# Queries and keys of a hybrid decoder trunk, transposed by VectorE blocks and a DRAM tile in place of TensorE

## The chip, the cores and the metric

The kernel runs on one core of a Trainium2 chip. The metric is the device time of one execution in microseconds (us); lower is better. The core has five engines with instruction queues of their own: TensorE (PE in the profile, its weight loads PEld), VectorE (DVE), ScalarE (ACT), GpSimd (POOL) and SyncE (SP). SP only issues DMAs here.

## The reference, cut to what matters

Two layers, each feed-forward, mixer, feed-forward, over 256 tokens of width 1024, all in float32. The part that the change touches is the attention of the mixer: eight heads of 128 columns.

```python
q, k, v, z, xbc, dt_raw, u, vg, gate_raw = jnp.split(xn @ w_in, split_at, axis=-1)
qt = (q * (dh ** -0.5)).transpose(0, 2, 1, 3)
...
s_own = jnp.einsum('bhqd,bhkd->bhqk', qb, k_own).astype(F32)
s_own = jnp.where(dist_own >= 0,
                  s_own - slopes[:, None, None] * dist_own.astype(F32), -jnp.inf)
...
p = jax.nn.softmax(scores, axis=-1).astype(vt.dtype)
```

With 256 tokens there is one key block, so the attention is plain causal attention with a distance penalty. The other two branches of the mixer are a state-space scan (SSD, 16 heads in two groups, chunks of 128 tokens) and a gated unit; the three are gated, projected and summed.

## The kernel before

**Tiling.** Tokens come in two tiles of 128 (`t` = 0, 1). Weights stream from DRAM in 496 blocks of 128 x 1024 float32 (`load`, line 160, into tile `raw`), six of them ahead. Each block is split by ACT into a rounded part `whi` (line 180) and by DVE into a rest `wlo` (line 181), eleven blocks ahead of their use, and each product is made of three matmuls (lines 213 to 215). Weights and their split take part in every stage, so a DVE instruction that stands still holds the splits behind it.

**Order.** A matrix product (`gemm`) issues its matmuls in a fixed order; after each piece it calls `pump` with that piece's time, and `tick` advances small side tasks (generators), each of which sleeps a number of microseconds from the table `W` after every `yield`. So the order of the instructions on every engine is fixed when the program is built. Each engine executes its own queue in order; an instruction that waits holds all behind it.

**The mixer around the change.** Products run in the order xbc, z, q (2 chunks of 512 columns), k (2 chunks), v (2 chunks), then the gates. `qk_evac` (line 730) is the side task of a q or k chunk: ACT copies the two 128 x 512 results out of PSUM into tiles `qtok` (line 504), and `transposed` (line 508) makes four TensorE transposes a token tile into a PSUM tile `ctr` (line 513), which ACT copies into `qT` or `kT` (line 516). The result has the head's 128 columns on partitions and the tokens along the free axis. Attention multiplies them (line 760, `qk`).

At the same time the scan runs (`ssd`, line 651). For each token tile and group it makes, per quarter of the heads, a weight tile `ssw`: a matmul `seg` (line 680), a DVE add (682), four ACT exponentials (686), a DVE product (688). Then eight matmuls `yd` (711) use two such tiles, and DVE adds their result to `y` (714, 722). `scaled` scales the values `xs` on DVE (671). After both groups `to_parts` transposes `y` on TensorE (`xtr`, 300), and DVE and ACT make the parts `xg`, `ysh`, `ysl` (314, 316, 317).

**Buffers.** Tiles of 128 x 512 come from one pool of six buffers, tag `b2` (line 54: `B4, B2 = 16, 6`). While the scan runs, three of the six are held throughout: `acsr` (the running sums, line 622), `btok` (line 560) and `cbt` (line 658). `qtok`, `ssw`, `xg` and the small helpers share the other three. When none is free, the next instruction that needs one waits for the last reader of the buffer that it is given. PSUM tiles of tag `tr` (`ctr`, `seg`, `yd`, `state`, `xtr`, `qk`) share three banks.

**What the feed-forward stages do.** There `swap_out` (line 275) lets DVE transpose every 32 x 32 block of a 128 x 512 tile in place (line 277, tile `xt`) and writes it to a DRAM tile; `swap_in` (line 282) reads it back with four DMAs that put the blocks where a whole transpose would have them. The weight columns are reordered on the host (`_woven`) so that each piece that is read is 128 floats long.

Of the kernel before, what the change touches and what calls it, by code (L numbers as in the profile page):

```python
# [9 lines left out]
F32 = mybir.dt.float32  # L10
# [6 lines left out]
P = 128  # L17
L = 2
S = 256
NT = S // P  # L20
# [31 lines left out]
def trunk(ctx, tc, a):  # L52
    nc = tc.nc
    V, A, G, T = nc.vector, nc.scalar, nc.gpsimd, nc.tensor
# [5 lines left out]
    dram = ctx.enter_context(tc.tile_pool(name="dram", bufs=1, space=bass.MemoryType.DRAM))  # L60
# [3 lines left out]
    def b4(name, shape=(P, 1024), dt=F32):  # L64
        return big.tile(list(shape), dt, name=name, tag="b4", bufs=B4)
# [216 lines left out]
    def swap_in(dst, rd):  # L282

        v = rd.rearrange("(a i) (c e) -> c i a e", a=4, c=4)
        for c in range(4):
            nc.sync.dma_start(dst[32 * c:32 * c + 32], v[c])

    def halves(ps, hi, lo):

# [188 lines left out]
    def mixer(l, x, r2, nxt):  # L478
# [29 lines left out]
        def transposed(toks, place, eng):  # L508

            for t in range(NT):  # L510
                ps = tr("ctr")
                for j in range(4):
                    T.transpose(ps[:, j * P:(j + 1) * P], toks[t][:, j * P:(j + 1) * P], ident)
                p3 = ps.rearrange("p (k t) -> p k t", k=4)
                if eng == "a":
                    A.copy(place(t), p3)
                else:
                    V.tensor_copy(place(t), p3)
                yield W["tr"]
# [208 lines left out]
        qk = {}  # L728

        def qk_evac(which, c, ps):  # L730
            toks = tokens(ps, rq if which == "q" else r2, "qtok")
            o = b4(f"{which}T", (P, 4, S))
            qk[which, c] = o
            yield W["qk"]
            yield from transposed(toks, lambda t: o[:, :, t * P:(t + 1) * P], "a")

        vv = {}

# [7 lines left out]
        def attention(yax, free):  # L746
            for t in range(NT):
                while t and not free:
                    yield 0
                n = (t + 1) * P  # L750
# [3 lines left out]
                for g in range(2):  # L754
                    sc[g] = (b4 if t else b2)("sc", (P, 4, n))
                    for u in range(0, 4, per):
                        ps = tr("qk")
                        for j in range(per):
                            hh = u + j
                            T.matmul(ps[:, j * n:(j + 1) * n], qk["q", g][:, hh, t * P:(t + 1) * P],  # L760
                                     qk["k", g][:, hh, 0:n], start=True, stop=True)
                        for j in range(per):
                            hh = u + j
                            V.scalar_tensor_tensor(sc[g][:, hh, :], alibi[t], 2.0 ** -(4 * g + hh + 1),
                                                   ps[:, j * n:(j + 1) * n], op0=ALU.mult, op1=ALU.add)
                        yield W["qs"]
                    V.reduce_max(mx[:, 4 * g:4 * g + 4], sc[g], axis=AX.X)
# [3 lines left out]
                for g in range(2):  # L771
                    for j in range(4):
                        c = slice(4 * g + j, 4 * g + j + 1)
# [7 lines left out]
                for g in range(2):  # L781
# [11 lines left out]
                    for j in range(4):  # L793
                        hh = 4 * g + j
# [187 lines left out]
    x, r2 = XT("x"), {}  # L982
# [73 lines left out]
def _woven(w, n):  # L1056

    v = w.reshape(*w.shape[:-1], -1, n // P, 4, 32)
    return np.ascontiguousarray(v.swapaxes(-3, -2)).reshape(w.shape)
# [27 lines left out]
def _arrays(i):  # L1087
    f = {k: np.ascontiguousarray(v, dtype=np.float32) for k, v in i.items()}
    w = f["w_in"]
    cut = np.cumsum([0, 1024, 1024, 1024, 1024, 1536, 16, 1024, 1024, 1024, 1024, 1024])  # L1090
    q, k, v, z, xbc, dt, u, vg, g0, g1, g2 = (w[:, :, s:e] for s, e in zip(cut[:-1], cut[1:]))
    order = [xbc, z, q, k, v, g1, f["p_ssm"], vg, g0, f["p_attn"], u, g2, f["p_sgu"], f["w_out"]]
    mix = [_chunks(m).reshape(L, -1, P, 1024) for m in order]
    col = lambda m: m.reshape(L, -1, P).transpose(0, 2, 1)
    par = np.concatenate(
        [col(f["ffn1_pre_g"]), col(f["mix_pre_g"]), col(f["ffn2_pre_g"]), col(f["ssm_norm_g"]),
         f["conv_w"].reshape(L, 4, CT, P).transpose(0, 3, 2, 1).reshape(L, P, 48),
         col(f["conv_b"]), f["sgu_b"].transpose(0, 2, 1)], axis=2)
    return {
        "x": f["x"].reshape(S, D),  # L1100
        "con": _constants(),
        "par": par.transpose(1, 0, 2),
        "hpar": np.stack([f["dt_bias"], f["a_log"], f["d_skip"]], axis=1),
        "gu1": _gated(f["ffn1_w_gu"]),
        "dn1": f["ffn1_w_down"].reshape(L, KF, P, D),
        "gu2": _gated(f["ffn2_w_gu"]),
        "dn2": f["ffn2_w_down"].reshape(L, KF, P, D),
        "mix": np.concatenate(mix, axis=1),
        "wdt": dt.reshape(L, KD, P, SH).transpose(0, 2, 1, 3).reshape(L, P, KD * SH),
        "sgw": f["sgu_w"].transpose(0, 1, 3, 2),  # L1110
        "ffn1_post_g": f["ffn1_post_g"],
        "mix_post_g": f["mix_post_g"],
        "ffn2_post_g": f["ffn2_post_g"],
        "sgu_ln_g": f["sgu_ln_g"],
        "sgu_ln_b": f["sgu_ln_b"],
    }
# [18 lines left out]
```

## Time and profile before

| | |
|---|---|
| median of 3 runs | 1486.49 us (1485.8 to 1487.09) |
| the profiled execution | 1487.98 us, of which the span of its instructions is 1486.2 us |
| PE busy | 1472.1 us, 99% of the span |
| PEld busy | 1218.8 us, 82% |
| DVE busy | 955.2 us, 64% |
| ACT busy | 782.6 us, 53% |
| POOL busy | 55.6 us, 4% |
| mean granted TensorE clock | 0.997 |
| DMA | 293.37 MB, mean 197 GB/s |

The span runs from the first to the last instruction of one profiled execution. A share of busy time is an average over stages; what holds the work up in one stage is read from the waits and the chain of that stage. In a row of a timeline stand start, time, engine, line, operation, output<-inputs, shapes, and in brackets the idle time of the engine before it with what ended that. An instruction of one engine can begin a little before the one ahead of it has ended, since they are pipelined, so distances from start to start count.

### The profile page before, as it was taken

To read this page: it belongs to the slowest core of one execution; us is meant where nothing else is said; L and a number is where in the kernel's file an instruction comes from. 1 tells how busy PE (TensorE), PEld (TensorE's weight loads), DVE (VectorE), ACT (ScalarE), POOL (GpSimd) and SP (SyncE) were. 2 spreads that over 40 slices of the span, in tenths; PEclk is the share of its full clock that TensorE was granted. 3 is DMA by queue.
4 is the path that set the end of the run, shared out by engine and by line. 5 is a ranking of instruction groups with operands and counts; after the bars stand their busy time and mean duration, and the time that the engine had idled before them with its cause. 6 is when DMAs were issued, how large, how long until landed. Compare 5 with 4: busy or idle time off the path is not lost.

```text
span 1486.2 us, 18786 instructions
## 1 busy us (share of the span) xinstructions
PE 1472.1 (99%) x6850; PEld 1218.8 (82%) x6850; DVE 955.2 (64%) x1160; ACT 782.6 (53%) x1079; POOL 55.6 (4%) x98
## 2 busy tenths in 40 slices
PE   9999999999999999999999999999999999999998
PEld 7888888878888888888888888888788888888886
DVE  6766477766666857656486564876665667676652
ACT  6644367555374536544364543765554645464441
POOL 0000020000000000000000000200000000000000
PEclk9999999999999999999999999999999999999999
DMA  8987655335556445888568784654354564478860
GB/s 291 323 253 236 199 190 179 127 115 184 159 181 217 168 154 198 283 230 259 163 230 256 235 253 132 224 167 135 119 192 141 194 204 170 134 272 261 238 200 29
DMA packets 112476, 293.37 MB, mean 197 GB/s; under 512 B 16896, under 2 KB 41600, under 8 KB 112384
## 3 DMA queue, kind: packets, MB, share of 16 engines
q1 hardware_dynamic: 111808, 291.84, 60.6%
q8 instruction: 54, 0.88, 0.2%
q10 hardware_dynamic: 576, 0.33, 0.1%
q14 instruction: 38, 0.31, 0.1%
HBM read 279.54 MB, written 12.58 MB: 197 GB/s over the span
## 4 chain that ended last, share of the span: by engine, by line
PE 94%; DVE 4%; ACT 1%; issue 1%; POOL 0%; DMA 0%; DVEq 0%; ACTq 0%; POOLq 0%
PE gu L213 11%; PE gu L215 11%; PE gu L214 11%; PE dn L213 5%; PE dn L215 5%; PE dn L214 5%; PE br L213 3%; PE br L215 3%; PE br L214 3%; PE gate L215 2%; PE gate L213 2%; PE gate L214 2%; DVE wlo L181 2%; PE xbc L215 1%; PE xbc L213 1%; PE xbc L214 1%
## 5 line engine op out<-in xcount | busy, mean ns | idle before, releaser
L181 DVE TENSOR_TENSOR wlo<-raw,whi 128x1024 fp32r<-128x1024 f32 x495 | 600.2, 1232 | 331.1 <-ACT whi L180 319.8
L180 ACT CAST whi<-raw 128x1024 fp32r<-128x1024 f32 x495 | 512.8, 1051 | 380.9 <-PE gu L215 131.8
L213 PE MATMUL gu<-whi,xh 128*128 128x512 f32 x704 | 276.0, 392 | 1.4 <-ACT xh L316 1.4
L214 PE MATMUL gu<-wlo,xh 128*128 128x512 f32 x704 | 274.9, 391 | 0.0
L215 PE MATMUL gu<-whi,xl 128*128 128x512 f32 x704 | 274.8, 390 | 0.0
L213 PEld LDWEIGHTS gu<-whi,xh 128*128 128x128 f32 x704 | 132.7, 188 | 29.8 <-ACT xh L316 1.8
L215 PEld LDWEIGHTS gu<-whi,xl 128*128 128x128 f32 x704 | 132.6, 188 | 28.0 <-DVE xl L317 0.4
L214 PEld LDWEIGHTS gu<-wlo,xh 128*128 128x128 f32 x704 | 132.5, 188 | 27.9 <-DVE wlo L169 0.9
L213 PE MATMUL dn<-whi,hTh 128*128 128x512 f32 x352 | 137.5, 391 | 0.0
L215 PE MATMUL dn<-whi,hTl 128*128 128x512 f32 x352 | 137.0, 389 | 0.0
L214 PE MATMUL dn<-wlo,hTh 128*128 128x512 f32 x352 | 136.9, 389 | 0.0
L215 PEld LDWEIGHTS dn<-whi,hTl 128*128 128x128 f32 x352 | 66.1, 188 | 13.8
L213 PE MATMUL gate<-whi,xh 128*128 128x512 f32 x192 | 77.3, 403 | 0.0
L214 PEld LDWEIGHTS dn<-wlo,hTh 128*128 128x128 f32 x352 | 66.1, 188 | 13.5
L213 PEld LDWEIGHTS dn<-whi,hTh 128*128 128x128 f32 x352 | 66.1, 188 | 13.4
L215 PE MATMUL gate<-whi,xl 128*128 128x512 f32 x192 | 75.0, 391 | 0.0
L214 PE MATMUL gate<-wlo,xh 128*128 128x512 f32 x192 | 74.8, 390 | 0.0
L316 ACT CAST xh<-xg 128x512 fp32r<-128x512 f32 (+1 forms) x25 | 15.1, 603 | 62.3 <-DVE xg L314 62.3
L215 PEld LDWEIGHTS gate<-whi,xl 128*128 128x128 f32 x192 | 36.0, 188 | 7.7
L405 ACT ACTIVATE silu<-gu,r 128x512 f32<-128x512 f32 (+1 forms) x48 | 31.3, 654 | 19.8 <-PE gu L215 16.2
L214 PEld LDWEIGHTS gate<-wlo,xh 128*128 128x128 f32 x192 | 36.2, 188 | 6.6
L213 PEld LDWEIGHTS gate<-whi,xh 128*128 128x128 f32 x192 | 36.1, 188 | 6.6
(243 smaller groups left out, 2248.3 us busy)
## 6 DMA issues: line engine op xcount, KB each, us to landing
raw<-in_mix SPq DMA_DIRECT2D x232, 512.0 KB, 4.2
raw<-in_gu SPq DMA_DIRECT2D x175, 512.0 KB, 4.9
raw<-in_dn SPq DMA_DIRECT2D x88, 512.0 KB, 4.5
swap<-xt SPq DMA_DIRECT2D x40, 256.0 KB, 3.2
hr<-swap SPq DMA_DIRECT2D x160, 64.0 KB, 4.9
row_ffn_post_g<-in_ffn_post_g SPq DMA_DIRECT2D x4, 512.0 KB, 7.0
swap<-xt SPq DMA_DIRECT2D x8, 128.0 KB, 4.4
hr<-swap SPq DMA_DIRECT2D x32, 32.0 KB, 6.1
```

The lines of the kernel that those rows point to most:

```text
L180: A.copy(hi, w)
L181: V.tensor_tensor(lo, w, hi.bitcast(F32), op=ALU.subtract)
L213: T.matmul(o, xh(k, t), hi[:, off:off + n], start=first, stop=False)
L214: T.matmul(o, xh(k, t), lo[:, off:off + n], start=False, stop=False)
L215: T.matmul(o, xl(k, t), hi[:, off:off + n], start=False, stop=last)
L316: A.copy(o_h, xg)
L405: A.activation(silu[t][:, :w], gate(t), AF.Silu, scale=r2[t])
```

## The change

Queries: after 2.6 us of sleep `swap_whole` lets DVE transpose the 32 x 32 blocks of both `qtok` tiles, writes them to one DRAM tile with eight DMAs (four a token tile) in runs of 32 floats, sleeps 6.5 us and reads the whole back into `qT` with one DMA. Keys: the columns of the key weights are woven on the host; the two tiles go out with `swap_out` and come back with `swap_in`, four DMAs a token tile, into a tile `kT` whose tokens lie in blocks of 32; the matmul of attention reads its keys through a view of 32-token pieces. The tiles `xt` come from the pool `b2`.

```diff
--- before.py
+++ after.py
@@ -284,6 +284,18 @@
         v = rd.rearrange("(a i) (c e) -> c i a e", a=4, c=4)
         for c in range(4):
             nc.sync.dma_start(dst[32 * c:32 * c + 32], v[c])
+
+    def swap_whole(toks, o):
+
+        rd = dram.tile([4, P, S], F32, name="swapw", tag="swapw", bufs=6)
+        v = rd.rearrange("k (c i) (t a j) -> t a i (k c) j", c=4, a=4, t=NT)
+        for t in range(NT):
+            xt = b2("xt")
+            V.transpose(xt, toks[t])
+            for b in range(4):
+                nc.sync.dma_start(v[t, b], xt[32 * b:32 * b + 32, :].rearrange("p (b j) -> p b j", j=32))
+        yield W["out"]
+        nc.sync.dma_start(o, rd.rearrange("k p e -> p k e"))
 
     def halves(ps, hi, lo):
 
@@ -729,10 +741,17 @@
 
         def qk_evac(which, c, ps):
             toks = tokens(ps, rq if which == "q" else r2, "qtok")
-            o = b4(f"{which}T", (P, 4, S))
-            qk[which, c] = o
-            yield W["qk"]
-            yield from transposed(toks, lambda t: o[:, :, t * P:(t + 1) * P], "a")
+            yield 2.6
+            if which == "q":
+                qk["q", c] = o = b4("qT", (P, 4, S))
+                yield from swap_whole(toks, o)
+            else:
+                o = b4("kT", (P, 2 * 4, 4, 32))
+                rd = [swap_out(x, 512) for x in toks]
+                yield W["out"]
+                for t in range(NT):
+                    swap_in(o[:, 4 * t:4 * t + 4].rearrange("p a k j -> p a (k j)"), rd[t])
+                qk["k", c] = o.rearrange("p b k j -> p k b j")
 
         vv = {}
 
@@ -758,7 +777,7 @@
                         for j in range(per):
                             hh = u + j
                             T.matmul(ps[:, j * n:(j + 1) * n], qk["q", g][:, hh, t * P:(t + 1) * P],
-                                     qk["k", g][:, hh, 0:n], start=True, stop=True)
+                                     qk["k", g][:, hh, 0:n // 32], start=True, stop=True)
                         for j in range(per):
                             hh = u + j
                             V.scalar_tensor_tensor(sc[g][:, hh, :], alibi[t], 2.0 ** -(4 * g + hh + 1),
@@ -1089,6 +1108,7 @@
     w = f["w_in"]
     cut = np.cumsum([0, 1024, 1024, 1024, 1024, 1536, 16, 1024, 1024, 1024, 1024, 1024])
     q, k, v, z, xbc, dt, u, vg, g0, g1, g2 = (w[:, :, s:e] for s, e in zip(cut[:-1], cut[1:]))
+    k = _woven(k, 512)
     order = [xbc, z, q, k, v, g1, f["p_ssm"], vg, g0, f["p_attn"], u, g2, f["p_sgu"], f["w_out"]]
     mix = [_chunks(m).reshape(L, -1, P, 1024) for m in order]
     col = lambda m: m.reshape(L, -1, P).transpose(0, 2, 1)
```

In the rows of the order below the text in brackets names the counters that the instruction waits for: PE, Activation, DVE and Pool are engines, DMAHW a transfer's landing.

The first place is PE in the first layer, where the second chunk of q is multiplied and the scan begins. Before:

```order
L513 MATMUL ctr_2491<-con_74,qtok_2439 128x128 [waits DVE_49,Activation_49]
L513 MATMUL ctr_2491<-con_74,qtok_2439 128x128 x3
L680 MATMUL seg_2497<-acsr_2417,sel_83 128x512 [waits Activation_49]
L702 MATMUL state_2506<-xw_2451,btok_2260 128x512 [waits DVE_49]
L213 MATMUL q_2432<-whi_2140,xh0_1619 128x512
L214 MATMUL q_2432<-wlo_2141,xh0_1619 128x512
L215 MATMUL q_2432<-whi_2140,xl0_1620 128x512
L213 MATMUL q_2432<-whi_2140,xh0_1619 128x512
L214 MATMUL q_2432<-wlo_2141,xh0_1619 128x512
L215 MATMUL q_2432<-whi_2140,xl0_1620 128x512
L513 MATMUL ctr_2521<-con_74,qtok_2441 128x128 [waits Activation_49]
L513 MATMUL ctr_2521<-con_74,qtok_2441 128x128 x3
```

With the change:

```order
L692 MATMUL seg_2504<-acsr_2417,sel_83 128x512 [waits DVE_49]
L714 MATMUL state_2513<-xw_2450,btok_2260 128x512 [waits DVE_49,Activation_49]
L213 MATMUL q_2432<-whi_2140,xh0_1619 128x512
L214 MATMUL q_2432<-wlo_2141,xh0_1619 128x512
L215 MATMUL q_2432<-whi_2140,xl0_1620 128x512
L213 MATMUL q_2432<-whi_2140,xh0_1619 128x512
L214 MATMUL q_2432<-wlo_2141,xh0_1619 128x512
L215 MATMUL q_2432<-whi_2140,xl0_1620 128x512
L213 MATMUL q_2452<-whi_2140,xh1_1706 128x512
```

The two groups of four transposes `ctr` are gone; `seg` and `state` of the scan follow each other.

The second place is DVE at the same time. Before:

```order
L181 TENSOR_TENSOR wlo_2461<-raw_2237,whi_2460 128x1024 [waits DMAHW7_49,Activation_49]
L682 TENSOR_TENSOR ssw_2475<-seg_2473,con_74 128x512 [waits PE_49]
L688 TENSOR_TENSOR ssw_2475<-ssw_2475,cbt_2449 128x512 [waits DVE_49,Activation_49]
L671 TENSOR_TENSOR xs0_2188<-xs0_2188,dt_2360 128x1024 [waits Pool_49]
L682 TENSOR_TENSOR ssw_2499<-seg_2497,con_74 128x512 [waits PE_49]
L688 TENSOR_TENSOR ssw_2499<-ssw_2499,cbt_2449 128x512 [waits DVE_49,Activation_49]
L181 TENSOR_TENSOR wlo_2510<-raw_2255,whi_2509 128x1024 [waits DMAHW0_49,Activation_49]
L181 TENSOR_TENSOR wlo_2534<-raw_2317,whi_2533 128x1024 [waits DMAHW1_49,Activation_49]
L181 TENSOR_TENSOR wlo_2552<-raw_2374,whi_2551 128x1024 [waits DMAHW2_49,Activation_49]
L714 TENSOR_TENSOR y0_2482<-yd_2564,y0_2482 128x512 [waits PE_49]
```

With the change (682 is 694 here, 688 is 700, 671 is 683, 714 is 726):

```order
L294 STREAM_TRANSPOSE xt_2473<-qtok_2439 128x512
L294 STREAM_TRANSPOSE xt_2479<-qtok_2441 128x512 [waits DVE_49]
L694 TENSOR_TENSOR ssw_2488<-seg_2486,con_74 128x512 [waits DVE_49,PE_49]
L700 TENSOR_TENSOR ssw_2488<-ssw_2488,cbt_2448 128x512 [waits DVE_49,Activation_49]
L683 TENSOR_TENSOR xs0_2188<-xs0_2188,dt_2360 128x1024 [waits Pool_49]
L694 TENSOR_TENSOR ssw_2506<-seg_2504,con_74 128x512 [waits DVE_49,PE_49]
L700 TENSOR_TENSOR ssw_2506<-ssw_2506,cbt_2448 128x512 [waits DVE_49,Activation_49]
L181 TENSOR_TENSOR wlo_2517<-raw_2255,whi_2516 128x1024 [waits DMAHW0_49,Activation_49]
L181 TENSOR_TENSOR wlo_2535<-raw_2317,whi_2534 128x1024 [waits DMAHW1_49,Activation_49]
L181 TENSOR_TENSOR wlo_2553<-raw_2374,whi_2552 128x1024 [waits DMAHW2_49,Activation_49]
L726 TENSOR_TENSOR y0_2495<-yd_2566,y0_2495 128x512 [waits PE_49]
L734 TENSOR_TENSOR y0_2495<-y0_2495,zs0_2159 128x512 [waits DVE_49]
```

Two block transposes now stand ahead of the first `ssw`, and the second `ssw` (`ssw_2506`) also waits for the first one's reads; the built program gives it the buffer of the first, `ssw_2488`.

The third place is DVE at the end of the scan's first token tile and the start of its second. Before:

```order
L714 TENSOR_TENSOR y0_2482<-yd_2668,y0_2482 128x512 [waits PE_49]
L722 TENSOR_TENSOR y0_2482<-y0_2482,zs0_2159 128x512 [waits DVE_49]
L181 TENSOR_TENSOR wlo_2693<-raw_2513,whi_2692 128x1024 [waits DMAHW6_49,Activation_49]
L314 TENSOR_TENSOR xg_2724<-xtr_2719,par_75 128x512 [waits PE_49]
L317 TENSOR_TENSOR ysl0_2718<-xg_2724,ysh0_2717 128x512 [waits Activation_49]
L181 TENSOR_TENSOR wlo_2729<-raw_2537,whi_2728 128x1024 [waits DMAHW7_49,Activation_49]
L314 TENSOR_TENSOR xg_2745<-xtr_2740,par_75 128x512 [waits PE_49]
L317 TENSOR_TENSOR ysl0_2718<-xg_2745,ysh0_2717 128x512 [waits Activation_49]
L682 TENSOR_TENSOR ssw_2757<-seg_2755,con_74 128x512 [waits PE_49]
L688 TENSOR_TENSOR ssw_2757<-ssw_2757,cbt_2449 128x512 [waits DVE_49,Activation_49]
L671 TENSOR_TENSOR xs1_2213<-xs1_2213,dt_2360 128x1024 [waits Pool_49]
```

With the change:

```order
L726 TENSOR_TENSOR y0_2495<-yd_2671,y0_2495 128x512
L734 TENSOR_TENSOR y0_2495<-y0_2495,zs0_2159 128x512 [waits DVE_49]
L181 TENSOR_TENSOR wlo_2696<-raw_2520,whi_2695 128x1024 [waits DMAHW6_49,Activation_49]
L326 TENSOR_TENSOR xg_2727<-xtr_2722,par_75 128x512 [waits DMAHW5_49,DMAHW4_49,DMAHW6_49,DMAHW3_49,PE_49]
L329 TENSOR_TENSOR ysl0_2721<-xg_2727,ysh0_2720 128x512 [waits Activation_49]
L181 TENSOR_TENSOR wlo_2732<-raw_2538,whi_2731 128x1024 [waits DMAHW7_49,Activation_49]
L326 TENSOR_TENSOR xg_2748<-xtr_2743,par_75 128x512 [waits DMAHW2_49,DMAHW1_49,DMAHW7_49,DMAHW0_49,PE_49]
L329 TENSOR_TENSOR ysl0_2721<-xg_2748,ysh0_2720 128x512 [waits Activation_49]
L277 STREAM_TRANSPOSE xt_2753<-qtok_2709 128x512
L277 STREAM_TRANSPOSE xt_2757<-qtok_2711 128x512 [waits DVE_49]
L694 TENSOR_TENSOR ssw_2769<-seg_2767,con_74 128x512 [waits DVE_49,PE_49]
L700 TENSOR_TENSOR ssw_2769<-ssw_2769,cbt_2448 128x512 [waits DVE_49,Activation_49]
```

Each of the two `xg` now waits for four landings of the DMAs that write `xt` to DRAM, and two block transposes of keys stand ahead of the `ssw` of the second token tile. Ahead of this piece, between the last `yd` of the first token tile and its `y0`, DVE now has two block transposes and two splits `wlo`, where before the splits stood earlier and `y0` came right behind `yd`.

On SP, eight issues of the query writes now stand between two loads of weights in each of the two q chunks, one read after three further loads, and two writes and eight reads for each k chunk.

## Rows read from the trace of the kernel before

**Rows 1.** The page: the chain that ended last, its share of the span by engine.

```profile
PE 94%; DVE 4%; ACT 1%; issue 1%; POOL 0%; DMA 0%; DVEq 0%; ACTq 0%; POOLq 0%
```

**Rows 2.** Who PE waited for, over the whole span: us in total, times, longest.

```profile
PE ctr L513 <- DVE ssw L682: 3.2, 2, 1.6
PE seg L680 <- DVE xg L314: 1.6, 2, 0.8
```

**Rows 3.** PE's instructions in order of time, first layer, around a group of transposes.

```profile
277.94 0.60 PE L513 MATMUL ctr<-con,qtok 128*128 128x128 f32 x4
278.29 0.48 PE L213 MATMUL q<-whi,xh 128*128 128x512 f32 x1
278.61 0.40 PE L214 MATMUL q<-wlo,xh 128*128 128x512 f32 x1
278.84 0.40 PE L215 MATMUL q<-whi,xl 128*128 128x512 f32 x1
```

**Rows 4.** The chain of work that ended last, from 300 to 322 us: start, time, what.

```profile
301.71 2.89 DVE wlo L181
...
310.05 0.61 DVE ssw L682
...
310.79 0.63 PE ctr L513 x4
...
311.88 0.24 PE k L215
312.11 0.42 PE k L213
...
315.10 0.43 PE k L214
315.52 0.23 PE k L215
```

**Rows 5.** A stretch of each layer: its bounds, length, busy time (and instructions) of PE, PEld, DVE, ACT, POOL, then granted clock, DMA share and GB/s.

```profile
312.00:316.00 4.00, 4.00 (x12) 3.15 (x11) 3.57 (x4) 1.78 (x5) 0.00 (x0) 0.57 0.02 1
...
1046.00:1050.00 4.00, 4.00 (x12) 3.11 (x12) 3.41 (x4) 1.97 (x4) 0.00 (x0) 0.59 0.01 2
```

**Rows 6.** DVE in order of time where the scan begins.

```profile
274.63 0.68 DVE L682 TENSOR_TENSOR ssw<-seg,con 128x512 f32<-128x512 f32 x1
276.72 0.69 DVE L688 TENSOR_TENSOR ssw<-ssw,cbt 128x512 f32<-128x512 f32 x1 [1.41 <-ACT ssw L686]
...
280.55 0.69 DVE L688 TENSOR_TENSOR ssw<-ssw,cbt 128x512 f32<-128x512 f32 x1 [1.41 <-ACT ssw L686]
281.97 1.23 DVE L181 TENSOR_TENSOR wlo<-raw,whi 128x1024 fp32r<-128x1024 f32 x1 [0.72 <-ACT whi L180]
283.40 2.36 DVE L181 TENSOR_TENSOR wlo<-raw,whi 128x1024 fp32r<-128x1024 f32 x2 [0.21 <-ACT whi L180]
```

**Rows 7.** DVE in order of time at the turn from the first token tile to the second.

```profile
298.05 0.69 DVE L714 TENSOR_TENSOR y<-yd,y 128x512 f32<-128x512 f32 x1 [0.68 <-PE yd L711]
...
304.52 0.68 DVE L314 TENSOR_TENSOR xg<-xtr,par 128x512 f32<-128x512 f32 x1
...
312.66 1.22 DVE L671 TENSOR_TENSOR xs<-xs,dt 128x1024 f32<-128x1024 f32 x1
313.80 1.22 DVE L181 TENSOR_TENSOR wlo<-raw,whi 128x1024 fp32r<-128x1024 f32 x1
314.93 0.69 DVE L682 TENSOR_TENSOR ssw<-seg,con 128x512 f32<-128x512 f32 x1
316.97 0.69 DVE L688 TENSOR_TENSOR ssw<-ssw,cbt 128x512 f32<-128x512 f32 x1 [1.35 <-ACT ssw L686]
```

**Rows 8.** PE in order of time: the three `yd` of the stretch, and what follows them.

```profile
283.87 1.89 PE L711 MATMUL yd<-xs,ssw 128*128 128x64 f32 x16
285.57 0.48 PE L680 MATMUL seg<-acsr,sel 128*128 128x512 f32 x1
...
296.12 1.89 PE L711 MATMUL yd<-xs,ssw 128*128 128x64 f32 x16
297.82 0.48 PE L213 MATMUL k<-whi,xh 128*128 128x512 f32 x1
...
319.70 1.89 PE L711 MATMUL yd<-xs,ssw 128*128 128x64 f32 x16
```

**Rows 9.** Groups of instructions: the block transposes of the feed-forward stages, and ACT's copies of keys out of `ctr`, and the longer `qk` matmuls.

```profile
L277 DVE STREAM_TRANSPOSE xt<-hh 128x512 f32<-128x512 f32 x40 | 25.9, 687 | 0.0
L516 ACT COPY kT<-ctr 128x512 f32<-128x512 f32 x8 | 4.5, 567 | 0.0
L760 PE MATMUL qk<-kT,qT 128*128 128x256 f32 x32 | 8.2, 378 | 0.0
```

**Rows 10.** DMA issues by kind: count, KB each, median us from issue to landing.

```profile
swap<-xt SPq DMA_DIRECT2D x40, 256.0 KB, 3.2
hr<-swap SPq DMA_DIRECT2D x160, 64.0 KB, 4.9
hr<-swap SPq DMA_DIRECT2D x32, 32.0 KB, 6.1
```

**Rows 11.** The write of the swapped tiles (line 279) and all their landings, least, median and most.

```profile
L279 SPq DMA_DIRECT2D swap<-xt x48: 326/327/1221, 41.0 to 1424.4; - x48
...
DMA to landing us min/median/max: 2.3/3.3/5.5
```

## The prediction, made before the result was known

> **What bounds the kernel now.** I read four views in this order. The page's chain by engine first: almost the whole end time is work of PE, and PE is busy 99% of the span, so only two things change the time, instructions that PE has to execute and moments at which PE stands still [rows 1]. Then the list of whom PE waited for, searched for lines that the change touches: two waits are of interest, `ctr` for DVE's `ssw` and `seg` for DVE's `xg`, each twice in the span, that is once a layer, 1.6 and 0.8 us long [rows 2]. Then the chain in the stretch around the first of them, which shows why it is there: `ctr`, `seg` and `yd` share three PSUM banks, and the transposes of a chunk of k wait until DVE has read `seg` into `ssw` [rows 4]. Last, the windows behind that wait: the granted clock, 0.997 over the whole span, is 0.57 and 0.59 in a stretch of 4 us right after it, in both layers, which is the lower of the two levels, 1.2 GHz, for most of the stretch [rows 5]. In the chain the matmuls of that stretch follow each other in 0.43 us (312.11 to 315.10 is seven of them), before and after in 0.23 us; with eight slow ones that is 8 x 0.20 = 1.6 us a layer [rows 4]. So a wait of PE costs its length, and at this place 1.6 us more.
>
> **What goes.** Eight groups of transposes leave PE in each layer (q and k, two chunks, two token tiles each). A group takes 0.35 us from its start to that of the next matmul, and the step behind it is 0.32 instead of 0.23 [rows 3]: 0.44 us, times 8 is 3.5 us a layer. With `ctr` gone, its wait of 1.58 us goes (half of 3.2), the stretch at the low clock behind it (1.6), and, with DVE and PE shifted against each other, the `seg` wait of 0.8 [rows 2, 4]. Together 3.5 + 1.6 + 1.6 + 0.8 = 7.5 us a layer, if nothing takes their place. ACT loses eight copies of 0.57 us a layer [rows 9] (the row counts those of k, four a layer), which helps nobody on the path, since ACT is half idle.
>
> **What comes: buffers.** DVE gets eight block transposes of 0.687 us a layer [rows 9], little on an engine that is 64% busy. Their tiles `xt` are what matters. They come from the pool of six, three of which the scan holds. With `xt` twice for each chunk beside `qtok` twice, the second `ssw` of the first yd group is given the buffer of the first `ssw`, as the order shows in its added wait. So it may be written only after the first four of the eight `yd` have read the first, and PE stands between fourth and fifth `yd` for the whole way that makes a weight tile. I go through what follows in one layer.
>
> (a) That wait. From the add of `ssw` to the end of its product DVE and ACT take 274.63 to 277.41 = 2.8 us [rows 6]. With a hand-over at both ends, of 0.13 us as from DVE's end 310.66 to `ctr` at 310.79 [rows 4], 3.0 us. This rests on the built order and needs no assumption on timing.
>
> (b) The next `seg` and `state` need a PSUM bank, and `state` gets the one that DVE frees by reading `yd` into `y`. On DVE three splits `wlo` now stand between the late product and `y`. After the product there are 0.72 us until ACT has the first `whi` [rows 6], then three splits at a spacing of 1.14 and `y` with 0.69 [rows 7]: 4.8 us. PE meanwhile has half of `yd` (0.85, from 1.70 for all, 283.87 to 285.57 [rows 8]), `seg` and six matmuls and the step to `state` (8 x 0.23): 2.7 us. PE waits 2.2 us. Here the three splits are what is queued between.
>
> (c) First `yd` of the second token tile needs the scaled `xs`. Before, `xs` ended at 313.88 and `yd` began at 319.70, a margin of 5.8 us [rows 7, 8]. PE now comes earlier by what it lost in between before, 1.6 + 1.6 + 0.8 and two groups of transposes, 4.9 us. DVE comes later: two block transposes of keys stand ahead of `ssw` (1.4), and behind the last `yd` of the first token tile stand two block transposes and two splits ahead of `y` (1.4 + 2.3 = 3.7, of which half a `yd`, 0.85, goes off because DVE is released halfway): 2.8. So 4.9 + 1.4 + 2.8 - 5.8 = 3.3 us of wait.
>
> (d) The same `yd`, second half: the second product ends 3.8 us after `xs` (313.88 to 317.66 [rows 7]), a split standing between; less the half `yd` 2.9 us.
>
> (e) After each of these two pairs of waits I expect the low clock as after the old wait, 1.6 us each; 1.1 of the first falls into PE's wait for `y` in (b): 2.1 us.
>
> Sum of what comes: 3.0 + 2.2 + 3.3 + 2.9 + 2.1 = 13.5 us; what goes is 7.5; so 6.0 us more a layer, 12 us in two layers. The profiled execution took 1487.98 us, so 1500.0; that execution lies 1.5 us above the median of the runs, which gives 1498.5.
>
> The Trainium skill, Perfetto Trace Analysis, section Optimization Strategy, says that gaps that come back at the same length on the engine that should be saturated can mean that SBUF or PSUM has no room for the next tile, and points at buffer counts. The trace agrees: the same two gaps appear in both layers [rows 2]. By that rule a change that takes two more of the six buffers adds gaps, which is what (a) does.
>
> **What I put at nothing.** SP issues in 0.33 us each [rows 11] and mostly waits for splits; weights are six blocks ahead, and the DMA engines have room. The weight splits are eleven blocks ahead, so that a DVE late by some 5 us doesn't reach the products through them. The `qk` matmuls read their keys in pieces of 32 columns: between nothing and double their time. Their 0.378 us [rows 9] overlap; by start to start a transpose of 128 columns takes 0.35 / 4 = 0.09 us [rows 3], so the 32 of 256 columns and the 32 of 128 take about 32 x 0.18 + 32 x 0.09 = 9 us, which is what a doubling would add. I take nothing: the columns are as many, and no row shows a price for how they lie. If keys come back in 7 us instead of 4.9 [rows 10], it is 1 us a layer.
>
> **Small writes.** The queries go out in runs of 128 B, which the trace of before doesn't have. DVE's `xg` gets a buffer that the write of `xt` must have left. From the end of the second transpose to `xg` there are two splits (2.3), then from `y` to `xg` 6.5 us as before (298.05 to 304.52 [rows 7]), or 2.5 if DVE has work to make up (two instructions of 0.69 and a split of 1.14 stand between); less 1.3 for four issues. So 3.5 to 7.5 us of cover. The nearest rows are the existing writes, 3.3 us and at most 5.5 [rows 11], 256 KB in one issue [rows 10], and the reads in pieces of 256 B, half the size of the others, which land in 6.1 against 4.9 us [rows 10]. I take 5 to 6 us, by the nearest of them, and a cover of 6 to 7, so no cost. At 10 us it is about 3 us a layer, at 15 about 8, all in waits of PE for `seg` or `xtr`. Below nothing it can't be, as nothing waits for these writes now.
>
> The Trainium skill, DMA: Bandwidth & Descriptors, section Specifications, asks for at least 512 B a transfer and says that below that the engine reads, modifies and writes. No run here shows a write to DRAM below 512 B; the 256 B reads point the same way [rows 10]. By that rule the landing, and with it the time, goes to the first rival.
>
> **Rivals.** First, slow landing: the 128 B writes take 10 to 15 us, `xg` waits for them on DVE, all behind it waits too, and PE stands in `seg`. For it: no row of such a write, and 256 B pieces are already slower. Against it: 64 KB a write on sixteen engines is little, and the margin is 3.5 to 7.5 us. Price 3 to 8 us a layer: 1504 to 1514.
>
> Second, which ends on the other side: DVE's lag is made up before it is needed. It is 64% busy, and if the splits of (b) to (d) find their `whi` ready and the scheduler's slack of 5.8 us in (c) stays, only (a) is left, 3.0 us a layer. Then 7.5 - 3.0 = 4.5 us a layer are won: 1486.5 - 9 = 1477.5, and 1471.5 is the least, if (a) were hidden too. Against it: splits stand by program order between product and `y`. It decides where the sum of (b) to (e) falls below 4.5 us a layer.
>
> Third, they cancel: (a) and (d) come, but no low clock; 7.5 against 5.9 to 7.5, 1483 to 1487.
>
> **How the numbers follow.** Forecast, slower by the waits for buffers: 0.69, with a range of its own of 1490 to 1504 (without (d) 3.1 us a layer, 1492.7, and a little below it; up to 9 us a layer, if the low clock lasts twice as long at one place and keys land late by 1 us). Slow landing, or the dear `qk` matmuls: 0.15. Lag made up: 0.11. Cancel: 0.05. From the same cases: faster by over 0.2% (3 us, about what a measurement of this kernel can tell from no change) 0.12, which is the lag made up and the end of the third; within it 0.06, the rest of the third and the low end of the forecast; slower 0.82. The range leaves out the faster case and the far end of the slow landing: 1488 to 1512.
>
> **What would show it.** In the changed profile: whom PE waits for has no `ctr`, but `yd` behind DVE's `ssw` product about 3 us once a layer and again at the second token tile, `state` for `y` 2 us, and `yd` for `xs`. If (a) holds, a timeline of PE shows the first `yd` split into two groups of eight with 3 us between. The clock windows show the low level behind those waits. If the small writes are slow, `xg` waits for a DMA and the landing of `swapw` is above 8 us. If `qk` in its row is above 378 ns, the layout costs. It would be wrong if PE's waits in `yd` and `state` sum to less than 4.5 us a layer.

## The result and the profile after

The changed kernel took 1502.95 us (median of 4 runs, 1502.22 to 1504.17), the kernel before 1486.79 us; the ratio is 1.0108, with a 95% interval of 1.0091 to 1.0126. It is 16 us slower; the forecast was 1498.5 us, 12 us slower. The profiled execution has a span of 1500.8 us, 14.6 us more than before.

The page's chain by engine, in the order of the engines of [rows 1]:

```profile
PE 91%; DVE 4%; ACT 2%; issue 2%; POOL 0%; DMA 0%; ACTq 0%; DVEq 0%; POOLq 0%
```

PE still makes up the chain, but its share has fallen by 3% of the span. The list of whom PE waited for (us in total, times, longest) says where that time went, beside [rows 2]:

```profile
PE yd L723 <- DVE ssw L700: 10.1, 4, 2.8
PE yd L723 <- DVE xs L683: 5.3, 2, 2.7
PE state L714 <- DVE y L726: 1.6, 2, 1.0
...
PE seg L692 <- DVE xg L326: 1.3, 2, 0.7
```

The `ctr` of queries and keys and its wait are gone. In its place stand three waits of `yd` a layer and one of `state`. PE in order of time, first layer, shows them in the brackets:

```profile
283.21 1.00 PE L723 MATMUL yd<-xs,ssw 128*128 128x64 f32 x8
287.04 1.10 PE L723 MATMUL yd<-xs,ssw 128*128 128x64 f32 x8 [2.82 <-DVE ssw L700]
287.95 0.48 PE L692 MATMUL seg<-acsr,sel 128*128 128x512 f32 x1
...
291.86 1.13 PE L714 MATMUL state<-xw,btok 128*128 128x512 f32 x2 [0.56 <-DVE y L726]
...
321.64 1.10 PE L723 MATMUL yd<-xs,ssw 128*128 128x64 f32 x8 [2.67 <-DVE xs L683]
325.38 1.97 PE L723 MATMUL yd<-xs,ssw 128*128 128x64 f32 x8 [2.65 <-DVE ssw L700]
```

The `yd` that was one row of sixteen at 283.87 [rows 8] is cut in two with 2.82 us between, and the one of the second token tile waits before each half. DVE shows what the first wait comes from:

```profile
279.18 1.22 DVE L683 TENSOR_TENSOR xs<-xs,dt 128x1024 f32<-128x1024 f32 x1
284.25 0.69 DVE L694 TENSOR_TENSOR ssw<-seg,con 128x512 f32<-128x512 f32 x1 [3.85 <-PE yd L723]
286.29 0.69 DVE L700 TENSOR_TENSOR ssw<-ssw,cbt 128x512 f32<-128x512 f32 x1 [1.35 <-ACT ssw L698]
287.71 3.50 DVE L181 TENSOR_TENSOR wlo<-raw,whi 128x1024 fp32r<-128x1024 f32 x3 [0.72 <-ACT whi L180]
291.12 0.69 DVE L726 TENSOR_TENSOR y<-yd,y 128x512 f32<-128x512 f32 x1
```

DVE stands idle for 3.85 us until the first half of `yd` has read the buffer: the two engines wait for each other in turn, DVE for the buffer and then PE for what DVE puts into it. The three splits ahead of `y` are there as well, and 286.29 to 291.81 is 5.5 us, of which 4.8 lie behind the product.

The clock is the larger surprise. Windows on the stretches at the low level (bounds, length, busy time and instructions of PE, PEld, DVE, ACT, POOL, then granted clock, DMA share and GB/s), beside [rows 5]:

```profile
288.50:291.90 3.40, 2.84 (x8) 1.70 (x6) 3.37 (x5) 1.08 (x2) 0.00 (x0) 0.51 0.52 154
322.60:329.40 6.80, 4.15 (x14) 2.89 (x13) 4.48 (x7) 4.32 (x8) 0.00 (x0) 0.50 0.42 142
1029.20:1036.00 6.80, 5.76 (x13) 3.35 (x12) 5.32 (x7) 3.00 (x8) 0.00 (x0) 0.50 0.80 252
1063.30:1073.50 10.20, 8.03 (x24) 6.31 (x25) 7.81 (x11) 4.32 (x8) 0.00 (x0) 0.50 0.48 151
```

The kernel before has two such stretches, 3.4 us each and PE busy all through. Now there are four, 27 us together, in which PE is busy 20.8 us. A product there takes nearly twice its time (0.43 us from start to start against 0.23, as in [rows 4]), so I count half of PE's busy time as lost: 10.4 us against 3.4 before.

### The profile page after: what moved, and what is told of

The parts are those of the page before. It is cut to its first block, busy times and chain, and to the rows that moved or that the text cites. A ratio compares the mean times of both kernels' runs of the same rounds, so it can differ in the third digit from the quotient of the medians.

```text
span 1500.8 us, 18795 instructions
## 1 busy us (share of the span) xinstructions
PE 1472.4 (98%) x6786; PEld 1216.3 (81%) x6786; DVE 964.4 (64%) x1176; ACT 776.3 (52%) x1063; POOL 55.8 (4%) x98
## 4 chain that ended last, share of the span: by engine, by line
PE 91%; DVE 4%; ACT 2%; issue 2%; POOL 0%; DMA 0%; ACTq 0%; DVEq 0%; POOLq 0%
PE gu L213 11%; PE gu L214 11%; PE gu L215 11%; PE dn L215 5%; PE dn L213 5%; PE dn L214 5%; PE br L215 3%; PE br L213 3%; PE br L214 3%; DVE wlo L181 2%; PE gate L213 2%; PE gate L215 2%; PE gate L214 2%; PE xbc L215 1%; PE xbc L213 1%
## 5 line engine op out<-in xcount | busy, mean ns | idle before, releaser
L213 PEld LDWEIGHTS dn<-whi,hTh 128*128 128x128 f32 x352 | 66.1, 188 | 13.5
L698 ACT ACTIVATE ssw<-ssw,nacs 128x128 f32<-128x128 f32 x64 | 20.6, 392 | 50.7 <-DVE ssw L694 50.7
L417 ACT ACTIVATE silu<-gu,r 128x512 f32<-128x512 f32 (+1 forms) x48 | 31.4, 655 | 19.9 <-PE gu L215 16.4
```

The costliest lines, as they stand in the source:

```text
L213: T.matmul(o, xh(k, t), hi[:, off:off + n], start=first, stop=False)
L417: A.activation(silu[t][:, :w], gate(t), AF.Silu, scale=r2[t])
L698: A.activation(w[:, j, :], w[:, j, :], AF.Exp, bias=st["nacs"][:, c:c + 1])
```

## The experiments

The waits come in different places for different reasons, so the runs undo one reason at a time. Every time stands beside runs of the kernel before on the same chip.

**A seventh buffer, in both kernels.** Theory: the wait in the first `yd` is for a buffer. Rival: DVE is late by its added transposes, and buffers don't matter.

```diff
-B4, B2 = 16, 6
+B4, B2 = 16, 7
```

> The changed kernel with seven buffers of tag b2 instead of six, nothing else. Theory (buffers in the first token tile, lateness of DVE in the second): the wait of 2.8 us between the two halves of the first yd goes in both layers, and so does the low clock that began right behind it (3.4 and 6.8 us long); PE's wait of state for y may grow to 1.7 us, since PE then comes earlier to it; the two waits in the yd of the second token tile (2.7 and 1.8 to 2.7 us) stay. 1503 - 2 x 2.8 - some 3 + 2 x 0.9 = about 1496. Rival (DVE is late by its block transposes, and buffers don't matter): the wait in the first yd stays at 2.5 us or more, time 1501 to 1504.

> The kernel before with seven buffers of tag b2, nothing else. Theory: nothing in the kernel before waits for a buffer of this tag on the path, since its waits (ctr for ssw, seg for xg) are for PSUM and for DVE: 1485 to 1488, with the same two waits. Rival (more buffers help any version, so what the changed kernel gained with seven says nothing on the change): 1478 to 1482.

The changed kernel took 1490.79 us, ratio 1.0027 (1.0017 to 1.0037), 12 us less than with six and 5 us less than the 1496 that I expected. The kernel before took 1487.0 us, 1.0007 (0.9998 to 1.0016), which is no change. PE's waits in the changed kernel with seven buffers:

```profile
PE yd L723 <- DVE xs L683: 5.3, 2, 2.6
PE yd L723 <- DVE ssw L700: 4.8, 2, 2.6
PE state L714 <- DVE y L726: 1.2, 2, 0.6
```

Of the four waits for the `ssw` product two are left, both in the second token tile; the one between the halves of the first `yd` is gone in both layers. The wait of `seg` for `xg` went too, which I had not expected, and `state` did not wait longer but 0.6 us. So the first wait is a buffer's, and the two of the second tile stay with one buffer more. An eighth was not run; in this trace DVE waits only 0.29 us a layer for a buffer that PE still reads.

**Queries alone, keys alone.** In one kernel only the queries take the new way, in the other only the keys.

```diff
             toks = tokens(ps, rq if which == "q" else r2, "qtok")
...
             if which == "q":
+                yield 2.6
                 qk["q", c] = o = b4("qT", (P, 4, S))
                 yield from swap_whole(toks, o)
             else:
-                o = b4("kT", (P, 2 * 4, 4, 32))
...
+                qk["k", c] = o = b4("kT", (P, 4, S))
+                yield W["qk"]
+                yield from transposed(toks, lambda t: o[:, :, t * P:(t + 1) * P], "a")
```

(The second kernel is the same with the two branches exchanged; the matmul `qk` and the woven columns follow the keys.)

> Only the queries go through the DRAM tile; the keys are transposed by TensorE as before. Theory: the wait in the first yd (2.8 us a layer) and that of state (0.6 to 1.0) are there as in the whole change, since they belong to the queries' tiles; in the second token tile the old waits of ctr and seg come back in some form (2.4 us a layer and a low clock behind them). From before: -3.5 for half the transposes, +2 x (2.8 + 0.8 + 2 of low clock) = +11: about 1494, 1490 to 1498. Rival (the keys' transposes ahead of ssw carry the loss): 1483, all transposes' gain of the queries and nothing lost.

> Only the keys go through the DRAM tile; the queries are transposed by TensorE as before. Theory: no wait in the first yd and none of state; in the yd of the second token tile the wait for xs falls from 2.7 to under 1 us (without the backlog that the queries' transposes leave on DVE), that in its second half stays at 1.8 to 3. From before: -3.5 for half the transposes, -8 for the old waits and their low clock, +2 x (0.7 + 2.6 + 2 of low clock): about 1486, 1482 to 1488. Rival (keys carry the loss): 1495 or more.

Queries alone: 1501.21 us, ratio 1.0099 (1.0084 to 1.0114). Keys alone: 1488.22 us, 1.0011 (1.0002 to 1.0021). Beside the kernel before's span of 1486.2 us, their spans of 1499.1 and 1487.8 are 12.9 and 1.6 us more, together 14.5, and the whole change has 14.6. By this the queries carry nearly all of it, but that the two add up is in part chance, since the waits are not the same ones. PE's waits with the queries alone:

```profile
PE yd L723 <- DVE ssw L700: 5.6, 2, 2.8
PE ctr L525 <- DVE xg L326: 4.2, 2, 2.1
PE ctr L525 <- DVE ssw L694: 2.9, 2, 1.6
```

The wait in the first `yd` is there unchanged, as the theory said; that of `state` shrank to 0.2 us in one layer, which it did not. The time lies above my range of 1490 to 1498: the block transposes of the queries leave DVE late at `xg`, and the `ctr` of the keys, which this kernel still has, waits 2.1 us for `xg`, where the kernel before had no wait of `ctr` for `xg`. These 7.1 us of `ctr` stand in place of the 9.8 us of the second token tile's `yd` in the whole change. With the keys alone the time lies 0.2 us above my range of 1482 to 1488. There is no wait in the first token tile, and the two of the second are 0.7 us for `xs` and 2.7 us for the second product:

```profile
PE yd L723 <- DVE ssw L700: 5.3, 2, 2.7
PE yd L723 <- DVE xs L683: 1.5, 2, 0.7
```

So `xs` is late by the queries' transposes of the token tile before (2.7 against 0.7 us), and the second product is late with the keys alone, because nothing but DVE's own chain lies between `xs` and it.

**The price of the clock.** Matmuls whose results are overwritten fill the places where PE waits, first twelve, then six.

```diff
                     for q in (2 * g, 2 * g + 1):
+                        if g == 0 and (t, q) != (0, 0):
+                            for _ in range(12):
+                                T.matmul(py[:, 256:512], ident, con[:, C_DIST:C_DIST + 256], start=True, stop=True)
                         for j in range(4):
```

> The changed kernel with twelve matmuls of 256 columns, whose results are overwritten, put where PE waits: between the halves of the first yd, ahead of the first yd of the second token tile and between its halves. They add work that the result doesn't need and take away nothing that PE waits for. Theory that the waits cost a second time through the clock: the stretches at 0.5 behind these places go (27 us of them in the span of the changed kernel, some 11 us lost), time 1491 to 1496. Rival (the low clock lies in time in which PE waits anyway): 1501 to 1505, or more by fillers that last longer than the waits.

> As filler, with six of the extra matmuls at each of the three places instead of twelve. In filler twelve lasted 5.24 us at a place where the wait is 2.7 to 2.8, so six should last 2.6 us and fill the wait without making it longer. Theory (the low clock behind the waits costs about 11 us in the changed kernel): granted clock 1.0 through the mixer, the waits in yd fall to some 0.2 us and time to 1490 to 1494. Rival (the low clock costs little, and filler was dear only by chance of its place): 1500 to 1504.

Twelve: 1505.45 us, ratio 1.0129 (1.0112 to 1.0146). Six: 1498.07 us, 1.0082 (1.0068 to 1.0096). Neither lies where the theory put it, and the first has the time that its rival gave for fillers longer than the waits; but it has it by the length of the fillers, as its profile shows. Windows over 60 us of each layer, with twelve:

```profile
280.00:340.00 60.00, 59.34 (x289) 49.68 (x289) 36.59 (x43) 26.57 (x51) 2.62 (x3) 1.00 0.52 145
1020.00:1080.00 60.00, 59.33 (x289) 49.70 (x288) 36.25 (x43) 26.85 (x52) 2.62 (x3) 1.00 0.58 157
```

and the same of the changed kernel:

```profile
280.00:340.00 60.00, 50.64 (x236) 40.48 (x236) 38.70 (x47) 29.05 (x54) 2.62 (x3) 0.91 0.53 154
1020.00:1080.00 60.00, 51.01 (x217) 40.25 (x216) 36.93 (x44) 27.84 (x53) 2.62 (x3) 0.86 0.52 150
```

The clock is full throughout. A row of PE gives the length of a filler:

```profile
284.30 5.40 PE L723 MATMUL yd<-con 128*128 128x256 f32 x24
289.54 1.00 PE L726 MATMUL yd<-xs,ssw 128*128 128x64 f32 x8
```

It is 5.24 us from start to start, nearly twice the wait. Six of these are 31.4 us; they take the place of 17.0 us of waits (`yd` 15.4, `state` 1.6), so without a gain by the clock the kernel would be 14.4 us slower than the changed one. It is 2.5 us slower. 11.9 us came back, and the windows had 10.4 for the clock. With six matmuls a place is 2.8 us long (320.62 to 323.43), but `state` then waits longer, and one stretch of 3.4 us a layer at the low clock remains behind it:

```profile
PE state L714 <- DVE y L729: 3.6, 2, 1.8
```

My range for six forgot that DVE is no faster: what PE spends in fillers, DVE's chain still has to end.

**Late DVE in the second token tile.** The first `yd` of that tile is issued later in the order, with seven buffers; in a second kernel the block transposes also come one step earlier.

```diff
-                    yield W["w2"]
+                    yield 10.4 if (t, g) == (1, 0) else W["w2"]
...
-            yield 2.6
+            yield 1.3
```

> The changed kernel with seven buffers, and the first yd of the second token tile issued 5.2 us of matmuls later in the order (a sleep of 10.4 instead of 5.2 us ahead of it). Theory (the two waits in that yd are there because DVE is behind PE as a whole, by some 5 us): the waits in yd shrink or go, and most of the time comes back as a wait of seg for y or yd right behind it, as DVE has as much left to do: 1486 to 1491, against 1490.8 without. Rival (only the place of this yd is wrong, and later in the order it costs nothing): all of it is won, 5 us of waits and 2 to 4 of low clock a layer, 1475 to 1479.

> As b7_late, and the block transposes of queries and keys one step earlier (a sleep of 1.3 instead of 2.6 us). A version that the theory says is quicker than both kernels: no wait between the halves of the first yd, state's wait under 0.5 us, and DVE behind PE by 1 to 2 us less in the second token tile: the gain of the transposes (7 us) stays, with one wait of 2 to 4 us a layer left and its low clock: 1477 to 1483. Rival (waits only change places and the loss stays as in b7): 1488 to 1491.

The first line alone: 1486.67 us, ratio 1.0003 (0.9994 to 1.0012). Both: 1478.81 us, 0.9949 (0.9936 to 0.9961), faster than both kernels. PE's waits with the first line:

```profile
PE seg L692 <- DVE y L726: 7.6, 2, 3.8
PE state L714 <- DVE y L726: 1.2, 2, 0.6
```

and with both:

```profile
PE seg L692 <- DVE y L726: 3.3, 2, 1.6
PE yd L723 <- DVE ssw L700: 1.6, 2, 0.8
```

A later `yd` turns two waits of together 5 us a layer into one of 3.8 us right behind it and wins 4.1 us: DVE is late as a whole, so most of the wait comes back. What wins more is to take work from ahead of it. One step earlier for the transposes does this (7.9 us more), and in this profile the clock stays at 1.00 from 280 to 340 us and from 1020 to 1080 us.

**The earlier step with six buffers.** Without the seventh buffer, and without or with the later `yd`.

> The changed kernel with a sleep of 1.3 instead of 2.6 us ahead of the block transposes, still six buffers. By the built order the second ssw then gets the buffer of the first xt, and waits for the four landings of its writes to DRAM instead of the four yd. Theory (which tile the second ssw inherits decides, not the number of buffers alone): no wait between the halves of the first yd, if the writes land in 3 us or less as in the changed kernel; state's wait 0.6 or less; the two waits of the second token tile stay at 2.6 to 2.8: 1489 to 1493, like seven buffers. Rival (six buffers are too few, whatever the order, or writes in 128 B runs land late here): a wait of 2 us or more in the first yd or in seg ahead of it, 1498 to 1504.

> As cand, with six buffers. Theory: as the second ssw waits for landed writes and not for yd, six buffers cost only what the later waits for buffers add (some 1 to 2 us a layer): 1480 to 1485. Rival (the seventh buffer makes the gain of cand): 1488 or more.

The earlier step alone: 1493.04 us, ratio 1.0037 (1.0025 to 1.0049), at the upper end of what the theory gave; the two waits of the second token tile fell to 2.3 and 2.0 us, where I had them stay. With the later `yd`: 1486.29 us, 0.9993 (0.9985 to 1.0002), between theory and rival: the seventh buffer is worth 7.5 us there, and not the 1 to 2 us a layer that I gave it. DVE in the kernel with the earlier step alone:

```profile
277.86 1.22 DVE L683 TENSOR_TENSOR xs<-xs,dt 128x1024 f32<-128x1024 f32 x1
279.00 0.69 DVE L694 TENSOR_TENSOR ssw<-seg,con 128x512 f32<-128x512 f32 x1
```

The second `ssw` follows `xs` without idle time. Six buffers are the same number as in the changed kernel; what differs is whose buffer it inherits, here by the built order that of a block transpose whose four writes to DRAM have landed. But `seg` now waits 1.8 us for `xg`:

```profile
PE seg L692 <- DVE xg L326: 3.6, 2, 1.8
```

**One account for all.** For each profiled execution I add up PE's waits in the mixer, half of PE's busy time in the windows at the low clock, the fillers, and 0.44 us for each group of transposes that is gone (7.0 us for all sixteen), and compare with the kernel before, whose own waits and clock are 4.8 + 3.4 = 8.2 us. Both layers, us:

| kernel | waits | low clock | fillers | transposes | sum, less 8.2 | span against before |
|---|---|---|---|---|---|---|
| changed | 18.3 | 10.4 | | -7.0 | +13.5 | +14.6 |
| seven buffers | 11.3 | 6.3 | | -7.0 | +2.4 | +3.3 |
| queries alone | 13.5 | 10.5 | | -3.5 | +12.3 | +12.9 |
| keys alone | 6.8 | 6.1 | | -3.5 | +1.2 | +1.6 |
| twelve fillers | 1.3 | 0 | 31.4 | -7.0 | +17.5 | +17.5 |
| seven buffers, later `yd` | 8.8 | 5.3 | | -7.0 | -1.1 | +0.2 |
| and earlier step | 4.9 | 0 | | -7.0 | -10.3 | -9.5 |
| earlier step, six buffers | 12.0 | 8.1 | | -7.0 | +4.9 | +5.3 |
| the same, later `yd` | 9.8 | 3.1 | | -7.0 | -2.3 | -1.7 |
| six fillers | 6.2 | 3.4 | 16.9 | -7.0 | +11.3 | +12.8 |
| before, seven buffers | 4.7 | 1.4 | | | -2.1 | -1.3 |

The sums lie 0 to 1.5 us below the spans, over a range of 27 us, so little is left for anything else of the change. The account says where the time went; what caused the waits rests on the runs above.

## Why the prediction was right, and where it was off

The direction, the mechanism and the places were right: PE's waits in `yd` and `state` are 8.5 us a layer, where under 4.5 would have refuted it. By its steps, two layers each:

- What goes. The transposes' 7.0 us are borne out by the account above. The wait of `ctr` (3.2) and the low clock behind it (3.4 in the windows) went. The wait of `seg` for `xg` did not: 1.3 of 1.6 us stayed. The prediction let it go by a shift of the two engines, though the backlog of its own step (c) stands ahead of `xg` as well. It goes with seven buffers.
- (a), the buffer: 2 x 3.0 forecast, 2 x 2.82 measured. The wait is at the place that the order named, and the seventh buffer takes it away.
- (b), `state`: 2 x 2.2 forecast (its own terms, 4.8 less 2.7, give 2.1), 1.6 in all measured. DVE's part was right (4.8 us from the end of the product to that of `y`). PE's part was not: 2.7 us were put down for its work until `state`, but the clock fell at about 288.5, and what I had as six matmuls at 0.23 went at half speed. From 287.04 to the start of the wait at 291.30 PE had 4.3 us of work. The wait was eaten by the clock, which is the same loss under another name.
- (c), `xs`: 2 x 3.3 forecast, 5.3 measured. With the keys alone 0.7 of the 2.7 us are left, so 2.0 go with the queries' part. Its backlog on DVE I had at 2.8, and it is 2.87: `y` begins 4.80 us behind the start of its `yd` (304.47 and 299.67), before 1.93 (298.05 and 296.12 [rows 7, 8]). PE stands 0.67 us of this in `seg` already.
- (d), the second product: 2 x 2.9 forecast, 2.65 and 1.80 measured.
- (e), the clock: this is the step that was mis-sized. I took one stretch of 3.4 us behind each pair of waits, as behind the old wait [rows 5], 4.2 us in two layers after an overlap; the windows show stretches of 3.4, 6.8, 6.8 and 10.2 us, 10.4 us lost, and the fillers gave back 11.9. The other runs show such lengths too: one wait of 1.8 us (`state`, six fillers) comes with 3.4 us at the low clock, one of 3.8 us (later `yd`) with 6.7 to 6.8, the pairs of 3.4 to 5.3 us with 6.7 to 10.2. But the length of a wait does not settle it: the same 2.8 us in the first `yd` comes with 3.4 us in one layer and 6.8 in the other, and in the kernel before with seven buffers the wait of `ctr` leaves the clock up in the first layer, in the stretch that had 0.57 in [rows 5]:

```profile
311.03 0.63 PE L513 MATMUL ctr<-con,qtok 128*128 128x128 f32 x4 [1.57 <-DVE ssw L682]
```

```profile
312.00:316.00 4.00, 4.00 (x19) 3.33 (x18) 3.56 (x4) 1.73 (x4) 0.00 (x0) 1.00 0.00 0
```

In its second layer the same wait comes with 3.4 us at the low clock. What decides whether the clock falls, and for how long, stays open.

Taken together (a) to (e) were 27 us in the forecast and are 27.4 in the trace: 0.4 us too much in (a), 2.8 in (b), 1.3 in (c) and 1.3 in (d), made good by 6 us too little in (e). The 2.8 of (b) came back as low clock; that the other errors cancel is luck. The rest of the distance to the measured 16 us is the `seg` wait that stayed (1.3), 1 us that the account doesn't cover, and that the runs lie 1.6 us farther apart than the two profiled spans.

The first rival, slow writes, fell. In the changed profile (KB each, median us from issue to landing; [rows 10] has the issues of before):

```profile
swapw<-xt SPq DMA_DIRECT2D x32, 64.0 KB, 2.4
qT<-swapw SPq DMA_DIRECT2D x4, 512.0 KB, 5.9
kT<-swap SPq DMA_DIRECT2D x32, 64.0 KB, 3.8
```

and DVE at the turn of the token tiles:

```profile
300.70 0.71 DVE L294 STREAM_TRANSPOSE xt<-qtok 128x512 f32<-128x512 f32 x1 [0.91 <-PE yd L723]
...
302.23 2.32 DVE L181 TENSOR_TENSOR wlo<-raw,whi 128x1024 fp32r<-128x1024 f32 x2
304.47 0.69 DVE L726 TENSOR_TENSOR y<-yd,y 128x512 f32<-128x512 f32 x1
...
310.94 0.68 DVE L326 TENSOR_TENSOR xg<-xtr,par 128x512 f32<-128x512 f32 x1
```

The small writes land in 2.4 us (1.8 to 3.6), inside the cover of 3.5 to 7.5 us that they were given, and `xg` comes 6.47 us behind `y`, as in [rows 7]: nothing on the path waits for them. The row of the Trainium skill (DMA: Bandwidth & Descriptors, section Specifications) that asks for at least 512 B for the line rate, and has the engine read, modify and write below that, would have led to 1504 or above by this way; these writes of 64 KB in runs of 128 B cost the kernel no such time. What they cost against writes of the same size in long runs, no run here shows.

The matmul of attention costs what it did, 378 ns in [rows 9] and here, and a row of four takes 0.67 us to the start of the next matmul in both kernels (395.94 to 396.61 before, 401.86 to 402.53 here), so keys in pieces of 32 columns are free:

```profile
L779 PE MATMUL qk<-kT,qT 128*128 128x256 f32 x32 | 8.2, 378 | 0.0
```

The second rival, DVE's lag made up in time, holds for none of the kernels with the transposes where the change put them. Its time is nearly reached with seven buffers, the transposes one step earlier and the `yd` later, 1478.8 against 1477.5, but by another sum: there (a) is gone, and 4.9 us of other waits are left. The third, waits without a low clock, fell with the windows.

The rule of the Trainium skill on gaps that come back at the same length (Perfetto Trace Analysis, section Optimization Strategy) held for one kind of them: a buffer more took away the first, and left the two of the second token tile, which appear in both layers too (2.7 us for `xs` in each, 2.7 and 1.8 us for the second product) and were DVE's lateness. A further buffer in the kernel before, which had gaps of the same kind, gave nothing.

The wait of `seg` for `xg`, 0.7 us with the change, gone with seven buffers and 1.8 us with the earlier step and six, follows how late DVE gets to `y`. In the changed kernel (the rows above) the block transposes of the second query chunk wait until `yd` has read the buffers that they get, then two splits follow. With the earlier step and six buffers they wait longer and three splits follow; with seven buffers only the second transpose waits:

```profile
295.63 0.71 DVE L294 STREAM_TRANSPOSE xt<-qtok 128x512 f32<-128x512 f32 x1 [3.07 <-PE yd L723]
...
297.16 3.45 DVE L181 TENSOR_TENSOR wlo<-raw,whi 128x1024 fp32r<-128x1024 f32 x3
300.53 0.68 DVE L726 TENSOR_TENSOR y<-yd,y 128x512 f32<-128x512 f32 x1
```

```profile
296.61 0.71 DVE L294 STREAM_TRANSPOSE xt<-qtok 128x512 f32<-128x512 f32 x1 [0.29 <-PE yd L723]
...
299.49 0.68 DVE L726 TENSOR_TENSOR y<-yd,y 128x512 f32<-128x512 f32 x1
```

Counted from the start of that `yd` (299.67, 294.59 and 295.58), `y` begins after 4.80 us with the change, 5.94 with the earlier step and 3.91 with seven buffers, and `seg` waits 0.67, 1.80 and nothing: one split more of 1.14 us is 1.13 us more of wait. So six buffers cost a second wait here besides (a).

## What to carry to other kernels

Work taken from the engine that is the bound is won only if the engine that takes it over is not late at the places where the bound engine waits for it; look in its queue for what stands ahead of the next handed-over tile, and count the tiles that the new work borrows from a shared pool. When a new wait appears, find out whose buffer the late instruction inherits: one more buffer, or the same number with the borrower one step earlier, each took away the same wait of 2.8 us, though the second left another wait for a buffer elsewhere. A wait of TensorE can cost more than its length where the clock falls behind it: here 18.3 us of waits came with 10.4 us lost at the low clock, so look at the granted clock behind every gap.

## What the runs showed that was not expected

Waits of 2.8 us or less came with up to 10.2 us at a granted clock of 0.5, and one place with 4.5 us of waits cost 4.0 us more by the clock (8.03 us of busy time in the last window). Twelve useless matmuls at three places a layer, 31 us in all, made the kernel only 2.5 us slower: they took the place of 17.0 us of waits and kept the clock at 1.00. Writes to DRAM in runs of 128 B, 64 KB each, landed in 2.4 us (2.0 to 3.3 in the other kernels that have them, by the median of each).
